# A row-wise maximum norm, one Trainium2 core: first tile loaded by partitions 0-15 and then 16-127, one joining reduction, pieces recut, last row by TensorE

## The chip, the cores and the metric

One core of a Trainium2 chip. The metric is device time in microseconds (us), median of two to seven executions. The runs were made on several chips; each is compared with the kernel before on the same chip in the same rounds. All runs were with a granted clock of 1.00. The profiled span is some 1.7 us shorter than the time reported. A change counts as faster or slower from 2% on, here 12.6 us.

## The reference

```python
def setup_inputs():
    return {"x": np.random.randn(8192, 8192).astype(np.float32)}

def reference(x):
    return np.linalg.norm(x, ord=np.inf, axis=1)     # per row: the largest |x|
```

256 MiB are read once, 32 KB are written. There is one pass of VectorE over every element.

## The kernel before

The 8192 rows are 64 blocks of 128. A block is loaded with one row on each partition, a pair of blocks with two neighbouring rows on each partition (16384 columns). `PIECES` says how blocks are cut by columns; the cuts get finer towards the end, so that little is left to do once the last byte is there. All tiles but the very last piece go through one ring of three pairs. Pairs are counted from 1 below; pair 24 is the first that is cut.

```python
HEAD = 4
PAIRS = 28
PIECES = (
    [[8192]] * HEAD
    + [[16384]] * 23
    + [[8192, 8192], [12288, 4096], [8960, 7424], [8704, 7680], [5504, 6016, 4864]]
    + [[4288, 3904], [3072, 2752, 2368], [2240, 2112, 1984, 1856]]
    + [[1984, 1664, 1472, 1152, 1088, 832]]
)
RING = 3 * 16384
...
    def join(row, n):                      # after each row block that came in parts
        nc.vector.tensor_reduce(
            out=res[:, row : row + 1], in_=part[:, row, :n], axis=mybir.AxisListType.X, op=MAX,
        )
...
            nc.sync.dma_start(out=buf, in_=src[:, off : off + w])      # one load a piece
...
    nc.vector.transpose(fin_t, fin)                                     # the last row block
    nc.sync.dma_start(
        out=out[(R - 1) * P :].rearrange("(b c) -> b c", c=32), in_=fin_t[0:P:32, :]
    )
```

(Cuts are marked by "..."; the reductions, the transposes through TensorE and the stores of finished rows are left out.)

## Time and profile before

| | |
|---|---|
| time | 632.03 us (631.86 to 632.37) |
| load queue busy | 98.8% of the span, mean 426 GB/s |
| VectorE busy | 553.5 us, 88% |
| VectorE idle | 74.0 us, all of it waiting for tiles of x, the last wait ending at 487.57 |
| first reduction | 13.37 us |
| last reduction | 626.60 us |

The first reduction says what the start costs. The last wait of VectorE says from where on nothing but VectorE's own work sets the end. The first reduction in the timeline of the kernel before (the bracket is the idle time before it and what ended it):

```profile
13.37 8.69 DVE L58 TENSOR_REDUCE res<-ring 128x1 f32<-128x8192 f32 x1 [13.37 <-DMA ring<-in_x_dram]
```

The GB/s row of the page, by fortieths of the span (15.8 us each):

```profile
GB/s 368 435 462 433 432 441 424 445 420 449 416 462 403 462 403 462 403 462 403 462 403 462 403 466 399 466 399 466 399 466 399 432 432 443 432 426 428 419 424 225
```

The first slice has 368 mostly since no packet of a load starts before 1.76 us (433 GB/s over the other 14.0 us would give 385, an estimate).

### The profile page before, as it was taken

How to read it: one execution, taken by the hardware profiler on the slowest of the kernel's cores; microseconds unless marked ns; L12 is line 12 of the kernel's file. 1: busy time of each engine (PE TensorE's matmuls, PEld its weight loads, DVE VectorE, ACT ScalarE, POOL GpSimd, SP SyncE). 2: the span in 40 equal slices, each digit the busy share in tenths (PEclk: the TensorE clock that was granted, in tenths of full speed). 3: DMA queues.
4: the chain of work that ended last, by engine and by line, in shares of the span. 5: the costliest groups of instructions: out<-in, count | busy, mean ns of one | idle time of the engine just before them, and what ended most of it. 6: DMA issues, size and time to landing. Idle time of an engine off the chain costs nothing. (4 is left out here: it accounts for less than half of the span.)

```text
span 630.5 us, 225 instructions
## 1 busy us (share of the span) xinstructions
PE 1.5 (0%) x4; PEld 0.4 (0%) x4; DVE 553.5 (88%) x66; ACT 2.3 (0%) x5; POOL 0.8 (0%) x7
## 2 busy tenths in 40 slices
PE   0000000000000000000000000000000000000000
PEld 0000000000000000000000000000000000000000
DVE  1983988889988889888898888898888999999998
ACT  0000000000000000000000000000000000000000
POOL 0000000000000000000000000000000000000000
DMA  8999999999999999999999999999999999999995
GB/s 368 435 462 433 432 441 424 445 420 449 416 462 403 462 403 462 403 462 403 462 403 462 403 466 399 466 399 466 399 466 399 432 432 443 432 426 428 419 424 225
DMA packets 7698, 268.49 MB, mean 426 GB/s; under 512 B 877, under 2 KB 912, under 8 KB 1936
## 3 DMA queue, kind: packets, MB, share of 16 engines
q1 hardware_dynamic: 7640, 268.44, 98.8%
q10 hardware_dynamic: 56, 0.03, 0.0%
q14 instruction: 2, 0.02, 0.0%
HBM read 268.44 MB, written 0.03 MB: 426 GB/s over the span
## 5 line engine op out<-in xcount | busy, mean ns | idle before, releaser
L58 DVE TENSOR_REDUCE res<-ring 128x2 f32<-128x16384 f32 (+1 forms) x32 | 473.9, 14818 | 74.0 <-DMA ring<-in_x_dram 74.0
L58 DVE TENSOR_REDUCE part<-ring 128x1 f32<-128x4096 f32 (+17 forms) x19 | 70.0, 3735 | 0.0
L58 DVE TENSOR_REDUCE last<-ring 128x1 f32<-128x1984 f32 (+4 forms) x5 | 8.0, 1676 | 0.0
L83 ACT COPY sb_pairs<-ps_pairs 28x128 f32<-28x128 f32 x2 | 0.5, 261 | 540.1 <-PE ps_pairs L82 540.1
L82 PE MATMUL ps_pairs<-ident,res 128*28 128x128 f32 x2 | 0.8, 395 | 539.8 <-DVE res L63 539.8
L63 DVE TENSOR_REDUCE res<-part 128x1 f32<-128x2 f32 (+2 forms) x8 | 1.2, 154 | 0.2
L72 ACT ACT_TABLE_LOAD x1 | 1.3, 1283 | 0.7 <-PEq L163 0.7
L58 DVE TENSOR_REDUCE fin<-last 128x1 f32<-128x837 f32 x1 | 1.0, 1025 | 0.1
L71 PE MATMUL ps<-ident,res 128*4 128x128 f32 (+1 forms) x2 | 0.7, 372 | 77.6 <-DVE res L58 51.3
L72 ACT COPY sb<-ps 4x128 f32<-4x128 f32 (+1 forms) x2 | 0.5, 254 | 76.1 <-PE ps L71 76.1
L82 PEld LDWEIGHTS ps_pairs<-ident,res 128*28 128x28 f32 x2 | 0.2, 104 | 540.4 <-DVE res L63 540.4
masks.py:199 POOL TENSOR_SCALAR_AFFINE_SELECT ident<-ident 128x128 f32<-128x128 f32 x1 | 0.3, 292 | 0.0
L144 DVE STREAM_TRANSPOSE fin_t<-fin 128x32 f32<-128x32 f32 x1 | 0.2, 211 | 0.0
L71 PEld LDWEIGHTS ps<-ident,res 128*4 128x4 f32 (+1 forms) x2 | 0.2, 81 | 77.9 <-issue 51.3
masks.py:197 POOL MEMSET ident<- 128x128 f32 x1 | 0.2, 204 | 0.3 <-POOLq L163 0.3
L55 POOL MEMSET fin<- 128x32 f32 x1 | 0.1, 124 | 0.0
L163 POOL MEMSET const-bfloat16-1.0<- 128x1 bf16 x1 | 0.1, 102 | 0.0
L163 POOL MEMSET const-uint8-127<- 128x1 uint8 x1 | 0.1, 102 | 0.0
L163 POOL MEMSET const-float32-0.0<- 128x1 f32 x1 | 0.1, 99 | 0.2 <-issue 0.2
L163 POOL MEMSET const-float32-1.0<- 128x1 f32 x1 | 0.1, 99 | 0.0
## 6 DMA issues: line engine op xcount, KB each, us to landing
ring<-in_x_dram SPq DMA_DIRECT2D x6, 4096.0 KB, 31.1
ring<-in_x_dram SPq DMA_DIRECT2D x1, 6144.0 KB, 36.0
ring<-in_x_dram SPq DMA_DIRECT2D x1, 4480.0 KB
ring<-in_x_dram SPq DMA_DIRECT2D x1, 4352.0 KB, 34.2
ring<-in_x_dram SPq DMA_DIRECT2D x1, 3840.0 KB
ring<-in_x_dram SPq DMA_DIRECT2D x1, 3712.0 KB
ring<-in_x_dram SPq DMA_DIRECT2D x1, 3008.0 KB
ring<-in_x_dram SPq DMA_DIRECT2D x1, 2752.0 KB, 41.2
```

The source lines that it names most:

```text
L55: nc.gpsimd.memset(fin, 0.0)
L58: nc.vector.tensor_reduce(out=dst, in_=src, axis=mybir.AxisListType.X, op=MAX, apply_absolute_value=True,)
L63: nc.vector.tensor_reduce(out=res[:, row : row + 1], in_=part[:, row, :n], axis=mybir.AxisListType.X, op=MAX,)
L71: nc.tensor.transpose(ps, res[:, r0 : r0 + n], ident)
L72: nc.scalar.copy(sb, ps)
L82: nc.tensor.transpose(ps, both[:, :, r], ident)
L83: nc.scalar.copy(sb[:, :, r], ps)
L144: nc.vector.transpose(fin_t, fin)
L163: nc = _bacc.Bacc("TRN2", target_bir_lowering=False, num_devices=1)
```

## The change

The intent: start all 16 DMA engines at once with a small first load, spend less on VectorE in the unbroken stretch at the end (one join for eight), save small stores, and end with one run of 512 bytes. Core of the diff:

```diff
-    + [[16384]] * 23
-    + [[8192, 8192], [12288, 4096], [8960, 7424], [8704, 7680], [5504, 6016, 4864]]
-    + [[4288, 3904], [3072, 2752, 2368], [2240, 2112, 1984, 1856]]
-    + [[1984, 1664, 1472, 1152, 1088, 832]]
+    + [[16384]] * 24
+    + [[7232, 9152], [6720, 9664], [8640, 7744], [5568, 5568, 5248]]
+    + [[4480, 3712], [3392, 1920, 2880], [2752, 1600, 2048, 1792]]
+    + [[1792, 1664, 1472, 1280, 1088, 896]]
...
-            nc.sync.dma_start(out=buf, in_=src[:, off : off + w])
+            if u == 0:
+                nc.sync.dma_start(out=buf[:16], in_=src[:16, off : off + w])
+                nc.sync.dma_start(out=buf[16:], in_=src[16:, off : off + w])
+            else:
+                nc.sync.dma_start(out=buf, in_=src[:, off : off + w])
...
-                if pending is not None:
-                    join(*pending)
-                    pending = None
...
+        if u == len(PIECES) - 2:
+            nc.vector.tensor_reduce(
+                out=res[:, CUT:], in_=part, axis=mybir.AxisListType.X, op=MAX,
+            )
+            pairs_out()
+            singles_out()
...
-    nc.vector.transpose(fin_t, fin)
-    nc.sync.dma_start(
-        out=out[(R - 1) * P :].rearrange("(b c) -> b c", c=32), in_=fin_t[0:P:32, :]
-    )
+    nc.tensor.transpose(fin_ps, fin, ident)
+    nc.vector.tensor_copy(out=fin_sb, in_=fin_ps)
+    nc.sync.dma_start(out=out[(R - 1) * P :].rearrange("(r p) -> r p", p=P), in_=fin_sb)
```

Two things that these cuts leave out: the row blocks are taken in another order (the pairs have the first 56, so the first tile is now block 56 and not block 0), and the single first tiles go through the joining reduction as well (15 row blocks of 4 values).

More of the change, by code (lines that the diff above doesn't have):

```diff
@@ L19 @@
     [[8192]] * HEAD
-    + [[16384]] * 23
-    + [[8192, 8192], [12288, 4096], [8960, 7424], [8704, 7680], [5504, 6016, 4864]]
-    + [[4288, 3904], [3072, 2752, 2368], [2240, 2112, 1984, 1856]]
-    + [[1984, 1664, 1472, 1152, 1088, 832]]
+    + [[16384]] * 24
+    + [[7232, 9152], [6720, 9664], [8640, 7744], [5568, 5568, 5248]]
+    + [[4480, 3712], [3392, 1920, 2880], [2752, 1600, 2048, 1792]]
+    + [[1792, 1664, 1472, 1280, 1088, 896]]
 )
 RING = 3 * 16384
+CUT = 48
+K = 4
 @with_exitstack
@@ L38 @@
     assert R == 64 and n_cols == 8192
+    X_ONE = 2 * PAIRS
     single = ctx.enter_context(tc.tile_pool(name="single", bufs=1))
@@ L43 @@
     ring = single.tile([P, RING], FP32)
-    res = single.tile([P, R], FP32)
-    part = single.tile([P, R, 8], FP32)
+    res = single.tile([P, R - 1], FP32)
+    part = single.tile([P, R - 1 - CUT, K], FP32)
+    nc.gpsimd.memset(part, 0.0)
     ident = single.tile([P, P], FP32)
@@ L52 @@
     last = single.tile([P, w_last + n_last], FP32)
-    fin = single.tile([P, 32], FP32)
-    fin_t = single.tile([P, 32], FP32)
-    nc.gpsimd.memset(fin, 0.0)
+    fin = single.tile([P, 1], FP32)
     def absmax(dst, src):
@@ L60, in absmax, with singles_out @@
         )
-    def join(row, n):
-        nc.vector.tensor_reduce(
-            out=res[:, row : row + 1], in_=part[:, row, :n], axis=mybir.AxisListType.X, op=MAX,
-        )
-    def rows_out(r0, n):
-        ps = psum_pool.tile([n, P], FP32, name=f"ps{r0}")
-        sb = single.tile([n, P], FP32, name=f"sb{r0}")
-        nc.tensor.transpose(ps, res[:, r0 : r0 + n], ident)
+    def singles_out():
+        n = R - 1 - X_ONE
+        ps = psum_pool.tile([n, P], FP32, name="ps_singles")
+        sb = single.tile([n, P], FP32, name="sb_singles")
+        nc.tensor.transpose(ps, res[:, X_ONE:], ident)
         nc.scalar.copy(sb, ps)
         nc.scalar.dma_start(
-            out=out[r0 * P : (r0 + n) * P].rearrange("(r p) -> r p", p=P), in_=sb
+            out=out[X_ONE * P : (R - 1) * P].rearrange("(r p) -> r p", p=P), in_=sb
         )
@@ L78, in pairs_out @@
         sb = single.tile([PAIRS, P, 2], FP32, name="sb_pairs")
-        both = res[:, HEAD : HEAD + 2 * PAIRS].rearrange("p (g r) -> p g r", r=2)
+        both = res[:, :X_ONE].rearrange("p (g r) -> p g r", r=2)
         for r in range(2):
@@ L84, in pairs_out @@
         nc.scalar.dma_start(
-            out=out[HEAD * P : (HEAD + 2 * PAIRS) * P].rearrange("(g p r) -> g p r", p=P, r=2),
-            in_=sb,
+            out=out[: X_ONE * P].rearrange("(g p r) -> g p r", p=P, r=2), in_=sb
         )
     at = 0
-    row = 0
-    pending = None
+    next_pair, next_one = 0, X_ONE
     for u, widths in enumerate(PIECES):
         k = sum(widths) // n_cols
+        if k == 2:
+            row, next_pair = next_pair, next_pair + 2
+        else:
+            row, next_one = next_one, next_one + 1
         src = x[row * P : (row + k) * P].rearrange("(p r) m -> p (r m)", r=k)
@@ L105 @@
                 at += w
-            nc.sync.dma_start(out=buf, in_=src[:, off : off + w])
+            if u == 0:
+                nc.sync.dma_start(out=buf[:16], in_=src[:16, off : off + w])
+                nc.sync.dma_start(out=buf[16:], in_=src[16:, off : off + w])
+            else:
+                nc.sync.dma_start(out=buf, in_=src[:, off : off + w])
             if final:
@@ L113 @@
                 left = n_cols - (off + s) % n_cols
-                if left == n_cols and w - s >= n_cols:
-                    c = (w - s) // n_cols
+                c = (w - s) // n_cols if left == n_cols else 0
+                if c and r + c <= CUT:
                     absmax(
@@ L127 @@
                 else:
-                    absmax(part[:, r, i : i + 1], buf[:, s:e])
-                if pending is not None:
-                    join(*pending)
-                    pending = None
-                if e - s == left and r < R - 1:
-                    pending = (r, i + 1)
+                    absmax(part[:, r - CUT, i : i + 1], buf[:, s:e])
                 s = e
             off += w
-        row += k
-        if row == HEAD + 2 * PAIRS + 1:
+        if u == len(PIECES) - 2:
+            nc.vector.tensor_reduce(
+                out=res[:, CUT:], in_=part, axis=mybir.AxisListType.X, op=MAX,
+            )
             pairs_out()
-            rows_out(0, HEAD)
-    assert pending is None
-    rows_out(HEAD + 2 * PAIRS, R - 1 - HEAD - 2 * PAIRS)
-    nc.vector.transpose(fin_t, fin)
-    nc.sync.dma_start(
-        out=out[(R - 1) * P :].rearrange("(b c) -> b c", c=32), in_=fin_t[0:P:32, :]
-    )
-    assert row == R
+            singles_out()
+    fin_ps = psum_pool.tile([1, P], FP32)
+    fin_sb = single.tile([1, P], FP32)
+    nc.tensor.transpose(fin_ps, fin, ident)
+    nc.vector.tensor_copy(out=fin_sb, in_=fin_ps)
+    nc.sync.dma_start(out=out[(R - 1) * P :].rearrange("(r p) -> r p", p=P), in_=fin_sb)
 _INS = ['x']
```

## The prediction

> **What bounds the kernel now.** I read the busy rows of the page first, then the stretches view (busy time and GB/s in chosen windows), then the timeline of the start and of the last 145 us, and last the landing times behind them. The queue that loads x was busy 98.8% of the span and VectorE 88%, so over the whole run the loads are the limit. From the page:
>
> ```profile
> PE 1.5 (0%) x4; PEld 0.4 (0%) x4; DVE 553.5 (88%) x66; ACT 2.3 (0%) x5; POOL 0.8 (0%) x7
> q1 hardware_dynamic: 7640, 268.44, 98.8%
> L58 DVE TENSOR_REDUCE res<-ring 128x2 f32<-128x16384 f32 (+1 forms) x32 | 473.9, 14818 | 74.0 <-DMA ring<-in_x_dram 74.0
> ```
>
> All of VectorE's idle time (74.0 us) is waiting for tiles of x. But it is not spread to the end. In the timeline, the bracket after a group is idle time before it and what ended it:
>
> ```profile
> 61.84 17.22 DVE L58 TENSOR_REDUCE res<-ring 128x2 f32<-128x16384 f32 x1 [10.67 <-DMA ring<-in_x_dram]
> 81.18 17.22 DVE L58 TENSOR_REDUCE res<-ring 128x2 f32<-128x16384 f32 x1 [2.13 <-DMA ring<-in_x_dram]
> ...
> 487.57 43.00 DVE L58 TENSOR_REDUCE res<-ring 128x2 f32<-128x16384 f32 x4 [2.13 <-DMA ring<-in_x_dram]
> 530.49 8.73 DVE L58 TENSOR_REDUCE part<-ring 128x1 f32<-128x4096 f32 x2
> 539.26 0.16 DVE L63 TENSOR_REDUCE res<-part 128x1 f32<-128x2 f32 x1
> ...
> 618.38 0.16 DVE L63 TENSOR_REDUCE res<-part 128x1 f32<-128x4 f32 x1
> 618.46 8.05 DVE L58 TENSOR_REDUCE last<-ring 128x1 f32<-128x1984 f32 x5
> ...
> 626.60 1.02 DVE L58 TENSOR_REDUCE fin<-last 128x1 f32<-128x837 f32 x1
> 627.66 0.21 DVE L144 STREAM_TRANSPOSE fin_t<-fin 128x32 f32<-128x32 f32 x1
> 627.90 0.65 SPq L145 DMA_DIRECT2D out_dram<-fin_t  x1
> ```
>
> A pair of row blocks (16384 columns) lands every 19.35 us and is reduced in 17.22 us, so VectorE waits 2.13 us each time. The last wait ends at 487.57, on pair 23. From there to 626.60 no line has a bracket: VectorE runs without a break for 139.0 us. The end is therefore **the landing of the last tile VectorE waits for, plus all VectorE work after it**. The loads themselves end earlier:
>
> ```profile
> 622.00:623.00 1.00, 0.00 (x0) 0.00 (x0) 1.00 (x2) 0.00 (x0) 0.00 (x0) 1.00 1.00 396
> 623.00:624.00 1.00, 0.00 (x0) 0.00 (x0) 1.00 (x2) 0.00 (x0) 0.00 (x0) 1.00 0.42 164
> 624.00:625.00 1.00, 0.00 (x0) 0.00 (x0) 1.00 (x2) 0.00 (x0) 0.00 (x0) 1.00 0.02 7
> ```
>
> (The last two columns are DMA share and GB/s.) The last piece is issued at 612.46 with 12.3 us to landing, so it is there at 624.7, and VectorE comes to it 1.9 us later.
>
> At the start, the first tile is issued at 0.74 and reduced from 13.37; later 8192-column tiles follow each other every 9.71 us. So 3.66 us of the first tile is start-up. In the packet records the first packet starts at 1.76; 11 of 16 engines have begun by 2.0, but the last begins only at 3.3. Each then takes 1.21 us per 32 KB row, in step, so this lag is in every later landing.
>
> [...]
>
> **The change part by part.**
>
> *Joins.* Starts on VectorE are n / 0.96 ns plus 60 ns apart. The reduce just before a join holds the engine some 116 ns more, since the join waits for it (4096 columns: 4.443 us instead of 4.327), and the join adds 72 ns: 188 ns each, seven of eight times, 0.12 for the other. That is 1.44 us on the unbroken stretch. After, one join of 60 elements per partition: 0.116 + 0.070 + 60/960 = 0.25 us. **-1.2 us.**
>
> *Recut.* Pair 24 was cut [8192, 8192] and is now whole. That moves the last wait. Pair 24 lands 19.35 us after pair 23 and VectorE is done with pair 23 after 17.14, so it waits once more: **+2.2 us** on the path. The number of data reductions behind is nearly the same (28 after, from pair 24; 30 before, from pair 23, which is one tile more), -0.06. Worked out in full: 487.57 + 19.35 = 506.92; columns from pair 24 to the last but one piece 114,688 - 896 = 113,792, / 0.96 = 118.53; 28 x 0.06 = 1.68; join 0.25; the wait before the last reduction 0.12. Sum 627.50, against 626.60: **+0.9 us** for joins and recut together. I ran the same sum over all pieces with loads at 1.178 ns per column + 0.06 us per transfer (fit to the 9.71 and 19.35): every piece of the new cut lands at least 2.5 us before VectorE gets to it, so no other wait appears; the old cut gave 2.0 us or more in the tail.
>
> *Last row.* The last reduction has 901 elements for 837: +0.07. Then, before: VectorE's transpose, 0.28 us from its end to the store's issue. After: TensorE (weights and pass, 0.40 as in the other transposes, with some 0.05 to start), a copy from PSUM of 128 elements[...], hand-overs of 0.03 each: 0.78. **+0.5 us.** The store has one 512 B run for four of 128 B; the old one landed 1.6 us after issue, and I allow the new one 0.1 less at most, and count nothing.
>
> *Stores.* One store for seven single rows in place of two, and the pairs' store, now all after the join at about 619.7. They have 8 us beside the last reductions; the old one from 619.29 was home by 623.5. 30 KB beside the last loads, which have over 2.5 us to spare. 0.
>
> *First tile in two.* [...]If that starts the late engines with the others, the slowest start moves from 3.3 to somewhere near 2.4, and every landing, pair 24's included, comes earlier. I choose **-0.6 us**: most of that lag, not all, as the second transfer must be prepared too.
>
> Sum: 632.03 + 0.9 + 0.07 + 0.5 - 0.6 = **632.9 us**.
>
> **The rivals.**
> 1. [...]The loads never get this back, as they are busy 98.8% of the time: 637 to 641 us. [...]Against it: somebody chose 16 for a tuned kernel[...]. I give it 0.35.
> 2. *A better start than thought.* The lag goes wholly, 1.3 us, and the transposed end costs 0.3: 632.0.
> 3. *The last wait is not on pair 24,* since loads at the end are slower than my line (from pair 23 to the end they took 137.2 us for 114,688 columns, 1.7 more than at the steady rate). With a margin of 2.5 us this needs a further loss; if it comes, the end follows the last landing and costs up to 1 us.
>
> **Range and chances.** [...]631.2 to 639.5[...]. 2% is 12.6 us; no part of the change that helps exceeds 1.5 us, so faster by 2% is next to impossible[...].
>
> **What would show it.** Right: a 2.1 us wait before pair 24's reduction near 506.5, then no gap to the end; one join of 0.2 us near 619; about 0.8 us from the last reduction's end to the last issue; the first reduction at 12.8. Wrong: [...]a wait for a load in the last 100 us; or no wait at pair 24.

The forecast was 632.03 + 0.9 + 0.07 + 0.5 - 0.6 = 632.9 us with a range of 631.2 to 639.5.

- In the +0.5 for the last row (0.78 us to the store's issue, for 0.28), the copy from PSUM was estimated. ScalarE's copies out of PSUM in the trace of before took 0.25 to 0.26 us; with 0.26 the terms come to about the 0.78.
- Under the -0.6, a load of 16 rows should start sooner. The trace of before has no such load, so the -0.6 was a guess. (Its "prepared too" is the second load's issue, 0.40 us in the trace after, from 1.19.)
- Rival 1, that a first load into few partitions is slow: its 637 to 641 us and its chance of 0.35. Without it the range was 631.2 to 634.

The 0.96 in the sums is measured: in the trace of before 16384 columns are reduced in 17.22 us and 8192 in 8.68, so 8192 more take 8.54 us, 0.96 columns a nanosecond.

## The result, and the profile after

The changed kernel takes **642.19 us** (642.03 to 642.58, five runs) against 632.03: a ratio of 1.0162, 95% interval 1.0148 to 1.0176. Ratios are the mean time of one kernel's fast runs over that of the other's of the same rounds, so not quite the ratio of the medians quoted. It is 10.2 us slower: below the 2% mark, far outside the noise, above the predicted range (631.2 to 639.5), and above the 641 at the top of rival 1.

The page of the changed kernel, the load queue and VectorE's two big groups (after the bar: busy us, mean ns of one; then idle time before and what ended it):

```profile
q1 hardware_dynamic: 7506, 268.44, 98.7%
L63 DVE TENSOR_REDUCE res<-ring 128x2 f32<-128x16384 f32 x24 | 413.3, 17220 | 59.7 <-DMA ring<-in_x_dram 59.7
L63 DVE TENSOR_REDUCE part<-ring 128x1 f32<-128x8192 f32 (+19 forms) x26 | 130.0, 5066 | 25.4 <-DMA ring<-in_x_dram 25.4
```

VectorE now waits 85.1 us for tiles (59.7 + 25.4) in place of 74.0, while the load queue is as busy as ever, 98.7%. Busy here means that packets were under way, not that they were quick. The GB/s row of the same page shows where they were not:

```profile
GB/s 215 369 428 430 459 442 409 450 401 459 450 401 454 430 426 450 401 459 446 405 450 405 454 450 401 459 434 418 450 401 459 446 392 436 435 428 427 418 423 200
```

The first slice fell from 368 to 215 and the second from 435 to 369; from the third on both swing about the same level. The timeline of the changed kernel, start and end:

```profile
22.43 8.69 DVE L63 TENSOR_REDUCE part<-ring 128x1 f32<-128x8192 f32 x1 [22.43 <-DMA ring<-in_x_dram]
...
496.52 17.22 DVE L63 TENSOR_REDUCE res<-ring 128x2 f32<-128x16384 f32 x1 [2.12 <-DMA ring<-in_x_dram]
515.88 17.22 DVE L63 TENSOR_REDUCE res<-ring 128x2 f32<-128x16384 f32 x1 [2.13 <-DMA ring<-in_x_dram]
533.01 95.27 DVE L63 TENSOR_REDUCE part<-ring 128x1 f32<-128x7232 f32 x22
628.32 0.22 DVE L138 TENSOR_REDUCE res<-part 128x15 f32<-128x60 f32 x1
628.45 7.98 DVE L63 TENSOR_REDUCE last<-ring 128x1 f32<-128x1792 f32 x5
636.46 1.09 DVE L63 TENSOR_REDUCE fin<-last 128x1 f32<-128x901 f32 x1
637.61 0.37 PE L146 MATMUL fin_ps<-ident,fin 128*1 128x128 f32 x1 [8.13 <-DVE fin L63]
638.02 0.28 DVE L147 COPY fin_sb<-fin_ps 1x128 f32<-1x128 f32 x1 [0.47 <-PE fin_ps L146]
638.33 0.31 SPq L148 DMA_DIRECT2D out_dram<-fin_sb  x1
```

The first reduction begins at 22.43, 9.06 us later than before. All later landings are later by about as much: pair 24 is reduced from 515.88, where before's spacing put it at 506.92. From there to the last reduction it takes 636.46 - 515.88 = 120.58 us without a gap, exactly as reckoned (627.50 - 506.92). So middle and tail went as predicted up to the last reduction; some 9 of the 10.2 us were lost in the first 22 us.

The stretches view of both kernels over that time (columns: window, then busy time of PE, PEld, DVE, ACT, POOL, then clock, DMA share, GB/s). Before:

```profile
6.00:22.00 16.00, 0.00 (x0) 0.00 (x0) 8.63 (x1) 0.00 (x0) 0.00 (x0) 1.00 1.03 446
24.00:40.00 16.00, 0.00 (x0) 0.00 (x0) 14.97 (x2) 0.00 (x0) 0.00 (x0) 1.00 1.00 432
```

and after:

```profile
6.00:22.00 16.00, 0.00 (x0) 0.00 (x0) 0.00 (x0) 0.00 (x0) 0.00 (x0) 1.00 0.91 248
24.00:40.00 16.00, 0.00 (x0) 0.00 (x0) 15.08 (x2) 0.00 (x0) 0.00 (x0) 1.00 1.00 430
```

The engines are occupied in both, but move 248 GB/s for 446 while the first tile is under way, and 430 for 432 once whole tiles follow. The packet records of the trace show it row by row. The first tile comes as 128 packets of 32 KB, one a row. The records do not name the engine, so I took the packets in order of start, sixteen at a time (as many as the page has DMA engines); their medians:

```
packet of the first tile       1     2     3     4     5     6     7     8    (us)
before, one load             1.82  1.23  1.21  1.21  1.21  1.21  1.21  1.21
after, 16 + 112 partitions   3.62  2.82  2.23  1.75  1.76  1.93  2.21  2.11
```

One thing went as intended: in the profiled run after, all 16 engines had begun by 2.10 us, before by 3.3. It bought nothing, as every packet then took longer.

A packet's recorded end is not yet its landing. The trace holds 16 semaphore counts for each load, and VectorE begins only after the last of them. Before, the last one of the first tile comes at 13.34 (the reduction begins at 13.37), 0.33 us after its last packet ended (13.01). After, the load into partitions 0 to 15 has its last packet end at 5.79 and lands at 7.44, 1.6 us later; the load into the other 112 ends at 21.28 and lands at 22.30, 1.0 us later. So the packet times in the table show only a part of the slowness. The views of the two issuing lines (109 and 110 of the kernel, issued at 0.74 and 1.19) give the same landings, in us from the issue:

```profile
DMA to landing us min/median/max: 6.7/6.7/6.7
DMA to landing us min/median/max: 21.1/21.1/21.1
```

### The profile page after: what moved, and what is told of

Read it like the earlier page. It is cut to its first block, busy times and chain, and to the rows that moved or that the text cites. A ratio compares the mean times of both kernels' runs of the same rounds, so it can differ in the third digit from the quotient of the medians.

```text
span 640.3 us, 217 instructions
## 1 busy us (share of the span) xinstructions
PE 1.2 (0%) x4; PEld 0.3 (0%) x4; DVE 552.7 (86%) x58; ACT 2.0 (0%) x4; POOL 0.8 (0%) x7
## 3 DMA queue, kind: packets, MB, share of 16 engines
q1 hardware_dynamic: 7506, 268.44, 98.7%
## 4 chain that ended last, share of the span: by engine, by line
DMA 60%; DVE 39%; SPq 0%; issue 0%; PE 0%
DMA ring<-in_x_dram 60%; DVE res L63 22%; DVE part L63 16%; DVE last L63 1%; DVE fin L63 0%; SPq L112 0%; SPq L110 0%; SPq L109 0%; PE fin_ps L146 0%; DVE fin_sb L147 0%; DVE res L138 0%
## 5 line engine op out<-in xcount | busy, mean ns | idle before, releaser
L63 DVE TENSOR_REDUCE res<-ring 128x2 f32<-128x16384 f32 x24 | 413.3, 17220 | 59.7 <-DMA ring<-in_x_dram 59.7
L63 DVE TENSOR_REDUCE part<-ring 128x1 f32<-128x8192 f32 (+19 forms) x26 | 130.0, 5066 | 25.4 <-DMA ring<-in_x_dram 25.4
L63 DVE TENSOR_REDUCE last<-ring 128x1 f32<-128x1792 f32 (+4 forms) x5 | 8.0, 1662 | 0.0
```

Of the source, the lines that this page charges most:

```text
L63: nc.vector.tensor_reduce(out=dst, in_=src, axis=mybir.AxisListType.X, op=MAX, apply_absolute_value=True,)
```

## The experiments

Theory A: the loss comes from which partitions are written at once. ("No loss" in run 6 and "no change" in run 8 are its branch; "memory side" is Theory C.) Theory B: any first tile in two loads costs this. Theory C: it comes from which rows are read at once from memory. Beside these: is the rest of the change worth +1.5 us as reckoned?

**1. One load for the first tile, all else as changed** (e_one_load)

```diff
-            if u == 0:
-                nc.sync.dma_start(out=buf[:16], in_=src[:16, off : off + w])
-                nc.sync.dma_start(out=buf[16:], in_=src[16:, off : off + w])
-            else:
-                nc.sync.dma_start(out=buf, in_=src[:, off : off + w])
+            nc.sync.dma_start(out=buf, in_=src[:, off : off + w])
```

> The changed kernel with the first tile loaded by one 128-partition transfer again; all else as changed. In the profile the first reduction came 9.06 us later than before (22.43 for 13.37) and all later landings by about 9.0. If the two-part load is the whole loss of the start: 642.2 - 9.0 = 633.2 us, and the first reduction at 13.4. If the recut or the late stores cost more than I reckoned (+0.9 and 0): 634 to 636.

Measured 632.78 us against 631.91 of before in the same rounds (ratio 1.0013, 0.9996 to 1.0029); first reduction at 13.06. The loss is gone with this one edit. What is left of the change costs 0.87 us, not the 1.47 that I had summed. The interval includes 1, so 0.87 is at the edge of what can be told, though each of the four times (632.73 to 632.80) lies above each of the seven of before (631.83 to 632.22).

**2. The kernel before with only that load split** (e_split_only): the same edit the other way round in the kernel before.

> The kernel before with only the first tile's load cut in partitions 0-15 and 16-127. If the cut alone makes the loss and everything later just moves: 632.0 + 9.0 = 641.0 us, first reduction at 22.4. If the loss needs the recut too, less than 637.

Measured 641.46 us (ratio 1.0150, 1.0134 to 1.0165), first reduction at 22.33. The split alone costs 9.55 us, and with the 0.87 of run 1 that makes 10.4, against 10.2 for the whole change: the parts add up within the spread of the runs.

**3. Changed kernel, one load, the old pieces** (e_old_cut): run 1 with `PIECES` of before.

> The changed kernel with one load for the first tile and the old pieces (pair 24 cut in two). Path from pair 23: 135.67 us of columns, 30 x 0.06, one join 0.25, wait 0.12 = 137.85, so the last reduction begins at 625.4 for 626.6 before, and if the transposed last row costs 0.5 before the store and gives 0.5 back in it: 630.8 us, better than both kernels. If the late last wait of the new cut were not on the path (rival), it would be as e_one_load.

Measured **630.50 us** (ratio 0.9978, 0.9963 to 0.9993): better than both kernels, if by 1.4 us only. The last reduction begins at 625.28. Against run 1 the old cut saves 2.28 us; the extra wait for pair 24 was reckoned at 2.2. In the timeline of run 1 that wait stands by itself:

```profile
506.57 17.22 DVE L63 TENSOR_REDUCE res<-ring 128x2 f32<-128x16384 f32 x1 [2.14 <-DMA ring<-in_x_dram]
523.71 43.16 DVE L63 TENSOR_REDUCE part<-ring 128x1 f32<-128x7232 f32 x7
```

and in that of run 3 the same place has no bracket, VectorE coming from pair 23 without a wait:

```profile
504.57 17.27 DVE L63 TENSOR_REDUCE res<-ring 128x1 f32<-128x8192 f32 x2
521.76 43.17 DVE L63 TENSOR_REDUCE part<-ring 128x1 f32<-128x8192 f32 x7
```

**4. The old end of the last row** (e_dve_last): run 3 with VectorE's transpose and the store of four runs of 128 bytes.

```diff
-    nc.tensor.transpose(fin_ps, fin, ident)
-    nc.vector.tensor_copy(out=fin_sb, in_=fin_ps)
-    nc.sync.dma_start(out=out[(R - 1) * P :].rearrange("(r p) -> r p", p=P), in_=fin_sb)
+    nc.vector.transpose(fin_t, fin)
+    nc.sync.dma_start(
+        out=out[(R - 1) * P :].rearrange("(b c) -> b c", c=32), in_=fin_t[0:P:32, :]
+    )
```

> e_old_cut with the old end of the last row: VectorE's transpose and four runs of 128 B, in place of TensorE, copy and one run of 512 B. From the traces: last reduction's end to the store's issue 0.28 us for 0.77, issue to the store's end 1.63 for 1.12. Sum equal: 630.5 us, within 0.2. If the transposed end were a loss of 0.5 as I predicted: 630.0.

Measured 630.69 us, against 630.50 of run 3, on another chip with the same 631.91 for before. Equal within the noise. The half microsecond that TensorE's way adds ahead of the store comes back in the store: its issue takes 0.31 us for 0.65, and from issue to its landing in the trace it takes 1.1 us for 1.6.

**5. Another split of the first tile: partitions 0-63, then 64-127** (e_64_64), on the kernel before.

```diff
+            if u == 0:
+                nc.sync.dma_start(out=buf[:64], in_=src[:64, off : off + w])
+                nc.sync.dma_start(out=buf[64:], in_=src[64:, off : off + w])
```

> The kernel before with the first tile's load cut in partitions 0-63 and 64-127. [...]If any first load in two parts costs the same whatever its partitions: 641. If the cause is that 16 neighbouring rows are read at once (memory side): [...]no loss: 632.

Measured 642.57 us (1.0168, 1.0153 to 1.0183). The packets' medians are 2.56 us in six of the eight steps, in both halves alike, for 1.21 in one load. The rate is less than half of the 446 GB/s before:

```profile
6.00:22.00 16.00, 0.00 (x0) 0.00 (x0) 0.00 (x0) 0.00 (x0) 0.00 (x0) 1.00 0.95 197
```

It cannot yet tell A from B (641 by B), and whether it speaks against C (632) depends on how the rows are dealt to the engines, which no run here shows for this split.

**6. The first tile split by columns** (e_cols): 1024 columns, then 7168, each on all 128 partitions, on the kernel before.

```diff
+            if u == 0:
+                nc.sync.dma_start(out=buf[:, :1024], in_=src[:, :1024])
+                nc.sync.dma_start(out=buf[:, 1024:], in_=src[:, 1024:w])
```

> The kernel before, first tile cut in two loads by columns (1024, then 7168), each on all 128 partitions. [...]no loss, 632 (631.3 to 632.7), first reduction at 13 to 13.8. Theory that any two-part first load costs: 641.

Measured 631.87 us (1.0000, 0.9985 to 1.0014). Here a first tile in two loads, both on all partitions, costs nothing, as Theory A had it:

```profile
6.00:22.00 16.00, 0.00 (x0) 0.00 (x0) 8.69 (x1) 0.00 (x0) 0.00 (x0) 1.00 1.01 435
```

Theory B falls. There is no gain in the time either, though all engines had begun by 2.16 us; the first reduction begins at 12.97, for 13.06 to 13.37 in the four profiled runs with one whole load.

**7 to 10. One extra small load ahead of the kernel before**, 16 rows of 32 KB, that differs in rows or partitions only. It goes to a part of the ring that is written over later, so the results stay right.

```diff
+    nc.sync.dma_start(out=ring[0:16,    32768:40960], in_=x[0:16, :])      # p_near
+    nc.sync.dma_start(out=ring[0:16,    32768:40960], in_=x[0:64:4, :])    # p_rows4
+    nc.sync.dma_start(out=ring[0:128:8, 32768:40960], in_=x[0:16, :])      # p_parts8
+    nc.sync.dma_start(out=ring[0:106:7, 32768:40960], in_=x[0:16, :])      # p_parts7
```

(One of the four lines in each.)

> The kernel before with one extra load ahead of all: 16 rows of 32 KB (rows 0 to 15) into partitions 0 to 15[...]. The result stays right, the data is written over later. In the changed kernel the same load's packets took 3.2 to 3.9 us. Expected the same here, and the first reduction some 2.5 to 3.5 us later than 13.37.

> As p_near, but rows 0, 4, ... 60 of x[...]; partitions 0 to 15 as before. [...]no change, packets 3.2 to 3.9 us. Memory side (neighbouring rows read at once): packets as in the usual start, 1.2 to 2.1 us.

> As p_near, rows 0 to 15, but into partitions 0, 8, ... 120[...]: packets about half as slow as p_near beyond the start-up, near 2.5 us (2.56 in the 64 + 64 run). Memory side: 3.2 to 3.9 us as p_near.

> As p_near, rows 0 to 15, but into partitions 0, 7, ... 105[...] all engines held up by the slowest: all near 2.5 us. Memory side: 3.2 to 3.9 us.

| run | partitions | rows | packets, us: least, median, most | first reduction | time, us (before 632.07) |
|---|---|---|---|---|---|
| p_near | 0-15 | 0-15 | 3.06, 3.59, 3.82 | 17.02 | 635.99 |
| p_rows4 | 0-15 | 0, 4, ... 60 | 3.06, 3.87, 4.44 | 17.24 | 636.29 |
| p_parts8 | 0, 8, ... 120 | 0-15 | 1.48, 2.14, 2.29 | 15.19 | 634.10 |
| p_parts7 | 0, 7, ... 105 | 0-15 | 1.61, 1.81, 2.34 | 15.28 | 634.06 |

Moving the rows apart makes nothing faster (a median of 3.87 us for 3.59); moving the partitions apart takes the packets from 3.6 to about 2 us, not far from the 1.82 of a usual start. The landings agree: the four loads are in by 7.48, 7.74, 5.50 and 5.57 us. For these 16 partitions theory A holds and C falls. p_near delays the first reduction by 3.65 us, just over the 2.5 to 3.5 expected. The packets of p_parts7 are not all near 2.5 us, and a little shorter than those of p_parts8 in the median (1.81 us for 2.14), but the load delays the first reduction as much (1.9 us; 512 KB at 433 GB/s would be 1.2, an estimate). Some 0.4 us of both delays is a later start: the first packet begins at 2.15 and 2.18, in p_near at 1.77. The issue took longer too: 0.58 to 0.65 us in p_parts8, p_parts7, p_fixed7 and the 64 + 64 run, for 0.4 where the first load went to 16 or 128 neighbouring partitions.

**11. The 112 partitions as seven loads** (e_seven), on the kernel before: 16 partitions, seven apart, in each.

```diff
+            if u == 0:
+                nc.sync.dma_start(out=buf[:16], in_=src[:16, off : off + w])
+                for j in range(7):
+                    nc.sync.dma_start(out=buf[16 + j : P : 7], in_=src[16 + j : P : 7, off : off + w])
```

> The kernel before, first tile as partitions 0-15, then the other 112 in seven loads of 16 partitions, seven apart (16+j, 23+j, ...). If the one 112-partition load deals each engine seven partitions in a row and in order, the engines get the very same rows in the same order here, and the time is that of e_split_only, 641 us, first reduction at 22.3. If it is dealt in another order, seven loads[...] (p_parts7 showed packets no slower than a usual start) take 1.2 to 1.7 us a step: first reduction at 16 to 18, 635 to 637 us.

Measured 641.20 us (1.0147, 1.0131 to 1.0162), first reduction at 22.49. Packet by packet it is e_split_only again (medians 3.68, 2.75, 2.26, 1.65, 1.85, 2.03, 2.26, 2.02 against 3.66, 2.66, 2.28, 1.65, 1.87, 1.97, 2.25, 2.08). So a load of 112 partitions deals each engine seven partitions in a row, in order, as far as equal packet times can show it. How a 128-partition load is dealt, no run here shows; its packets take a steady 1.21 us.

**12. A tiny first load** (p_wake): 16 partitions, 512 bytes each, ahead of the kernel before.

```diff
+    nc.sync.dma_start(out=ring[0:16, 32768:32896], in_=x[0:16, 0:128])
```

> The kernel before with a tiny load ahead of all (16 partitions, 512 B each). If the late start of single engines (up to 3.3 us in the run of before, 2.7 in e_old_cut) is a cold start which a first small load takes away: first reduction at 12.5 to 12.9, 631.3 us. If it comes with dealing out 128 rows: no gain, 632 to 632.5.

Measured 632.50 us (1.0009, 0.9994 to 1.0024). Its 16 packets were done by 1.97 us, but the tile's packets still began between 2.22 and 3.16. A small load ahead does not make the big one start evenly; it only comes first.

**13. The 112 partitions from other rows** (e_rows112): e_split_only with `in_=x[0 : 4 * 112 : 4, ...]` for the second load. The first tile's result belongs to other rows. (That the engines read 7 rows apart in e_split_only follows from run 11.)

> e_split_only, but the 112 partitions are loaded from rows 0, 4, 8, ... 444 of x, so that the engines read 28 rows apart instead of 7 (the first tile's result is wrong on purpose). If the slow 112-partition steps (1.65 to 2.8 us a packet) come from where the rows lie in memory, the first reduction moves away from 22.3 by more than 1 us. If from where the partitions lie: unchanged, 22.3, 641.4 us.

Measured 641.33 us against 631.95, first reduction at 22.53, packet medians 3.67, 2.81, 2.27, 1.73, 1.77, 1.96, 2.24, 2.10: the same pattern again. The place of the rows does not matter here either. Theory C falls for the 112 partitions too. Theory A is left for them by exclusion (the rows here, the second load in run 6, the number of loads in run 11); no run wrote them in another order to get the speed back.

**14. Four loads to one fixed set of partitions** (p_fixed7), 16 x 16 KB each, ahead of the kernel before.

```diff
+    for j in range(4):
+        lo = 32768 + j * 4096
+        nc.sync.dma_start(
+            out=ring[0:106:7, lo : lo + 4096],
+            in_=x[16 * (j // 2) : 16 * (j // 2) + 16, (j % 2) * 4096 : (j % 2) * 4096 + 4096],
+        )
```

> The kernel before with four extra loads of 16 x 16 KB ahead, all into partitions 0, 7, ... 105[...]. A 16 KB packet takes 0.61 us at the usual rate.[...] All engines coupled[...]: all 16 near 0.9 to 1.2 us.

Measured 636.87 us against 631.95, first reduction at 18.09. By order of start, the 16 packets of the second load took 0.61 to 0.97 us (median 0.79), those of the third 0.81 to 1.38 (1.05), and those of the fourth, already mixed with packets of the first tile, 0.75 to 1.44 (1.00). The usual 0.61 is an estimate, half of the 1.21 us that 32 KB take in whole tiles. The medians of the third and the fourth lie in the 0.9 to 1.2 expected with all engines held up, that of the second does not. The landings are plainer. The four loads land at 3.64, 4.84, 6.04 and 6.86 us (medians of their 16 counts), so the second and the third 1.20 us after the one before, twice 0.61. So loads into these 16 partitions, seven apart, are slow as well when they follow each other. Why is **open**. Nor do the runs explain the uneven steps of the 112 partitions: in run 11, where each of the seven steps is a load of its own, they land (medians) 2.20, 2.15, 1.46, 1.82, 2.38, 2.10 and 2.12 us after the step before. The third and the fourth are the quickest, and so they are in the packets of the other three runs with this split. That is a pattern and not yet a rule; no run was made to test what makes it.

## Why the prediction was wrong, point by point

**The step that failed** is "First tile in two", put down as -0.6 us. It costs +9.55 us (run 2): loaded 16 + 112, the first tile of the changed kernel lands at 22.30 and not at 13.34, since its packets take 1.75 to 3.62 us for 1.21 to 1.82 and land later after their end. That a load into few partitions may be slow had been named as rival 1, but with a chance of 0.35, and it was sized at 637 to 641, on figures that no run here shows; the range then ended at 639.5. The argument that carried the choice, that somebody chose 16 for a tuned kernel, is no measurement, and it lost.

**Within that loss**, the landings say which of the two loads costs more. The 16 partitions: the packets are recorded with 3.62 us, but the load lands at 7.44, where the first row of one whole load would have landed near 4.9 (an estimate: the last first packet ended at 4.54, and the first tile's last landing came 0.33 after its last packet): 2.6 us. The 112 partitions: from 7.44 to their landing at 22.30 it is 14.9 us for 7 x 1.21 = 8.5, so 6.4. The two make up the 9.0 by which the landing is late, and the 112 partitions are most of it.

**The gain hoped for** was not there. The two-load start did bring all engines in by 2.10 us (2.10 to 2.46 in the six profiled runs that begin with 16 rows into partitions 0-15), but in runs 6 and 12, where no slow load into few partitions hides it (run 12's is 512 bytes a partition), an early small load gained nothing: 631.87 and 632.50. The late engine of the profiled run before (3.3 us) was partly chance: the four profiled runs with one whole load showed 2.3 to 3.3.

**Joins and recut, +0.9:** right. 120.58 us from pair 24 to the last reduction, as reckoned to the hundredth. The recut's share, 2.2, measured 2.28 (run 3 against run 1). Joins alone: the last reduction of run 3 begins 137.8 us after pair 23's, for 139.0 before, so -1.2 as reckoned. The last wait is on pair 24; rival 3 did not occur.

**Last row, +0.5:** the 0.78 us to the store's issue was right (637.55 to 638.33), the sum wrong. I counted nothing for the shorter store and it gave 0.5 back; run 4 shows the two ends equal. This is most of why run 1 costs 0.87 and not 1.47. The copy from PSUM took 0.28 us, close to the 0.25 to 0.26 of ScalarE's in the trace of before.

**Stores, 0:** right. Both are issued by 630.6 and cause no gap.

Sum of what the runs show: 9.55 (split) + 0.87 (all else) = 10.4, against 10.2 measured.

## What to carry to other kernels

If a load has to be cut, try columns before partitions: two loads on all 128 partitions cost nothing here (631.87 us for 631.91), two on 16 + 112 or 64 + 64 cost 9.5 to 10.7 us for a single 4 MiB tile. In this kernel, whose load queue is busy 98.7% of the span, the loss at the start was not made good, and the DMA share (0.91 and 0.95 in that stretch, at 248 and 197 GB/s) hardly reveals it: read GB/s beside it, and the landings beside the packets. Before recutting pieces, find the last wait of the engine that follows, and add up its work from there; that sum was right to a tenth of a microsecond.
